# Finished output blocks of a streaming layer: the sample frames' transfers move from ScalarE's queue to SyncE's

## The chip, the cores and the metric

The kernel runs on one core of a Trainium2 chip. The metric is the device time of one execution, in microseconds (us). Engines are named as the profile names them: PE is the matmul engine (PEld its weight loads), DVE the vector engine, ACT the scalar engine (ScalarE), POOL the GpSimd engine, SP the engine that here only issues DMA transfers (SyncE). An ACTq or SPq row is an instruction that one of these sequencers handles itself, such as the issue of a DMA; while ACT's sequencer issues or waits, ACT's computing instructions behind it wait too.

## The reference, cut to what matters

One layer, fp32: a prompt of 512 frames and 64 further frames of a running stream (the sample), 2048 channels each. The time of this change lies in the last matrix product, the down projection, and in writing its result plus the residual to two separate outputs.

```python
def hybrid_layer(x, k_past, v_past, conv_past, ...):
    hn = rmsnorm(x, g_norm1)
    proj = hn @ w_in                                # q, k, v and three convolution groups
    ...                                             # stick-breaking attention, gated convolution
    x = x + mix @ w_out
    h2 = rmsnorm(x, g_norm2)
    x = x + (jax.nn.silu(h2 @ w_gate) * (h2 @ w_up)) @ w_down     # 5632 -> 2048 channels
    return x, k, v, new_conv
...
    yp, kp, vp, cp = hybrid_layer(yp, kp0, kp0, cp0, *wts)                       # 512 frames
    ys, kn, vn, cn = hybrid_layer(ys, cache_k[l], cache_v[l], state_conv[l], *wts)   # 64 frames
```

## The kernel before, in words

Prompt and sample are worked on together, as one block of 576 frames (512 + 64) that lies transposed on the chip: channels on the 128 partitions, frames along the free axis, in two halves of 288 frames. Each fp32 matrix product is made of three matmuls of rounded parts (high times high, low times high, high times low). Weights are loaded raw by DMA from SP's queue (`load_columns`, line 1418), rounded by ACT (line 222, a CAST into `whl`) and their remainder taken by DVE (line 223).

The gate, up and down projections are split into units. A unit multiplies a 2 x 2 block of weights (column halves c = 0, 1) by a 2 x 2 block of frames (halves i = 0, 1) with seven products instead of eight, numbered p_ = 1 to 7 (`run`, `multiply`, line 1532). The partial sums live in PSUM tiles named psy, psw and psx. ACT copies the intermediate state of psy to SBUF (`kept`, line 1542, the tile `part`), and PE's next product into the same psy tile waits for that copy. DVE adds products into the accumulators `acc` (line 1562), POOL adds the copied parts (line 1564).

The down projection has eight column blocks d of 256 output channels and is cut along its 5632 inputs into 37 units (`DOWN`). The list `order` fixes the sequence of products. After each product, the weights of the product four places later are prepared (`AHEAD = 4`). The last eight units finish the column blocks in the order d = 0, 1, 3, 6, 7, 5, 2, 4.

When a unit is the last one of its column block, `store_y` writes the finished accumulators out. It has two ways:

- All column blocks but the last (d = 4) use `turn_blocks`: nine steps after the accumulator is done DVE transposes it in place, 32 x 32 at a time (line 1731), and two steps later `blocks` issues its transfers (line 1720). A full accumulator (576 frames) gives four transfers of 64 KB for the prompt (line 1720, on SP's queue) and four of 8 KB for the sample (the same line, on ACT's queue), one for each group of 32 partitions. Column block 5 has its halves apart: the first half gives four of 36 KB, all prompt, the second four of 28 KB for the prompt and four of 8 KB for the sample. Each transfer moves pieces of 128 bytes.
- The last unit (d = 4) uses `work`: PE transposes the accumulator (lines 1739 and 1742), ACT copies it back (lines 1744 and 1748), and the transfers go out by SP's queue, with the remaining rows by ACT's queue (lines 1700, 1702, 1750, 1755).

From the last up unit on, the program order of ACT, DVE, SP and POOL is the written one, that of PE from the start: each engine works through its own list in order, and an instruction that waits holds everything behind it on that engine. On SP's list the transfers of line 1720 stand between the loads of weights (line 1418) and of hidden activations; on ACT's list they stand between the CASTs of line 222 and the copies of line 1542.

Of the kernel before, what the change touches and what calls it, by code (L numbers as in the profile page):

```python
# [17 lines left out]
TP = 512  # L18
# [76 lines left out]
def tile_hybrid_stream_step(  # L95
# [6 lines left out]
    nc = tc.nc  # L102
# [5 lines left out]
    yp, ys = y_prompt[0], y_sample[0]  # L108
# [151 lines left out]
    def misc(name):  # L260
        return ps_z.tile([P, 512], F32, tag="misc", name=name, bufs=2)
# [219 lines left out]
    t1 = tc.alloc_tile_pool(name="t1", bufs=1, reuse_waits="tile", side="left")  # L481
    dg = t1.tile([P, 5, P], F32, tag="vtok", name="dg")
    for i in range(5):
        n = P if i < 4 else TS
# [692 lines left out]
    for k_, (n, p_) in enumerate(corder):  # L1177
# [7 lines left out]
        if n == NCU - 1 and p_ in (6, 7, 4):  # L1185
            q = {6: 1, 7: 2, 4: 3}[p_]
            t = bt["pool"].tile([P, NH, 2, HALF], F32R, tag=f"t{q}", name=f"forms{q}")
# [430 lines left out]
    for d, v in visits.items():  # L1618
        n = next(a for a, b in zip(v, v[1:]) if a >= NGU + 10 and b >= a + 4)
# [70 lines left out]
    def store_y(n, c, i):  # L1690

        d = UNITS[n][1]
        src, cs, f0 = acc[d, c, i], slice((2 * d + c) * P, (2 * d + c + 1) * P), HALVES[i][0]
        r = HALF - 2 * P

        def put(f, ap, q=nc.sync):

            rows, n_p = ap.shape[0], max(min(TP - f, ap.shape[0]), 0)
            if n_p:
                q.dma_start(out=yp[f : f + n_p, cs], in_=ap[:n_p])  # L1700
            if n_p < rows:
                q.dma_start(out=ys[f + n_p - TP : f + rows - TP, cs], in_=ap[n_p:])

        lone = (d, c) not in both
        k0 = 0 if lone or i == 0 else r
        rest = None
        if lone:
            rest = src[:, 2 * P :], f0 + 2 * P
        elif (d, c) in one:
            rest = both[d, c].rearrange("p i t -> p (i t)")[:, 2 * P : 2 * P + 2 * r], 2 * P  # L1710
        one[d, c] = i

        def blocks(f, ap):

            n = ap.shape[1]
            n_p = max(min(TP - f, n), 0)
            for y, t0, t1, g, eng in ((yp, 0, n_p, f, nc.sync), (ys, n_p, n, f + n_p - TP, nc.scalar)):
                for q in range(4 if t1 > t0 else 0):
                    b0 = cs.start + 32 * q
                    eng.dma_start(out=y[g : g + t1 - t0, b0 : b0 + 32].rearrange("(b t) c -> t b c", t=32),  # L1720
                                  in_=ap[32 * q : 32 * (q + 1), t0:t1].rearrange("t (b c) -> t b c", c=32))

        def turn_blocks():
            if (d, c) in both:
                if done.setdefault((d, c), i) == i:
                    return
                all_, f = both[d, c].rearrange("p i t -> p (i t)"), 0
            else:
                all_, f = src, f0
            yield 9  # L1730
            nc.vector.transpose(out=all_, in_=all_)
            yield 2
            blocks(f, all_)

        def work():
            yield 4
            po = misc("pot")[:, : 3 * P]
            for q in range(2):
                nc.tensor.transpose(po[:, q * P : (q + 1) * P], src[:, k0 + q * P : k0 + (q + 1) * P], ident)
            if rest:  # L1740
                nr = rest[0].shape[1]
                nc.tensor.transpose(po[:nr, 2 * P :], rest[0], ident)
            ob = src[:, k0 : k0 + 2 * P].rearrange("p (i c) -> p i c", c=P)
            nc.scalar.copy(out=ob, in_=po[:, : 2 * P].rearrange("p (i c) -> p i c", c=P))
            if rest:
                turn[0] += 1
                obs = late["raw"][: 2 * r, 4096 + turn[0] % 4 * P : 4096 + (turn[0] % 4 + 1) * P]
                nc.scalar.copy(out=obs[:nr], in_=po[:nr, 2 * P :])
            if i == 0:
                nc.sync.dma_start(out=yp[: 2 * P, cs].rearrange("(i p) c -> p i c", p=P), in_=ob)  # L1750
            else:
                put(f0 + k0, ob[:, 0, :])
                put(f0 + k0 + P, ob[:, 1, :])
            if rest:
                put(rest[1], obs[:nr], nc.scalar)

        pipe.spawn(work() if n == NU - 1 else turn_blocks())
# [107 lines left out]
```

## Time and profile before

Three runs took 2373.28, 2369.54 and 2368.44 us.

| what | before |
|---|---|
| median of the three runs | 2369.54 us |
| the profiled execution, whole | 2369.07 us |
| its span in the trace | 2367.0 us |
| PE busy in the span | 2340.9 us (99%) |
| DVE, ACT, POOL busy | 82%, 49%, 12% |
| granted clock of PE | 1.0 |
| transfers of line 1720 on ACT's queue | 56 (32 + 12 + 4 + 4 + 4) |

The trace starts its clock with the span; 2.07 us of the profiled execution lie outside it. A row of the timeline gives start, duration, engine, line, operation, what it writes and reads, the count of merged instructions, and in square brackets the idle time of that engine before it and what ended it. A row of waits gives the total, the number and the longest wait.

### The profile page before, as it was taken

The page shows a single profiled execution, that of the slowest core. Times are in us where ns is not written, and L with a number is a line of the kernel's source. Part 1 is how long each engine was busy: PE and PEld are TensorE (multiplying, and loading weights), DVE is VectorE, ACT ScalarE, POOL GpSimd, SP SyncE. Part 2 cuts the span into 40 slices and gives each one's busy share as a digit, 9 for nine tenths or more (in the row PEclk, how much of TensorE's full clock was granted, in tenths as well). Part 3 has the DMA queues.
Part 4 walks back from the last instruction along what each step waited for, and adds up shares of the span by engine and source line. Part 5 has one row for each costly group of instructions (what it writes and reads, how often), then busy time and mean ns, then how long its engine had stood idle before and what let it go on. Part 6 is the DMA issues. An engine that isn't in the chain of part 4 may idle for free.

```text
span 2367.0 us, 43888 instructions
## 1 busy us (share of the span) xinstructions
PE 2340.9 (99%) x17581; PEld 2329.5 (98%) x17581; DVE 1935.3 (82%) x2908; ACT 1156.0 (49%) x2039; POOL 294.5 (12%) x386
## 2 busy tenths in 40 slices
PE   8999999999999999999999999999999999999998
PEld 8999999999999999999999999999999999999998
DVE  7878777788887889888888888888888777887896
ACT  6656655444444555444444444444444444444443
POOL 1011111341111230000000000000000002431221
PEclk9999999999999999999999999999999999999999
DMA  8466544684368654444444444444444936885553
GB/s 259 128 175 169 139 138 112 217 266 126 110 226 227 194 166 154 137 152 136 139 152 135 140 152 134 141 152 133 142 152 132 356 115 208 221 235 199 190 143 85
DMA packets 588804, 395.74 MB, mean 167 GB/s; under 512 B 100030, under 2 KB 577720, under 8 KB 588600
## 3 DMA queue, kind: packets, MB, share of 16 engines
q1 hardware_dynamic: 574776, 375.93, 50.9%
q0 software_dynamic: 8624, 16.22, 3.4%
q8 instruction: 137, 2.24, 0.4%
q10 hardware_dynamic: 5200, 0.79, 0.2%
q14 instruction: 67, 0.55, 0.1%
HBM read 301.45 MB, written 91.44 MB: 166 GB/s over the span
## 4 chain that ended last, share of the span: by engine, by line
PE 89%; DVE 5%; DMA 2%; ACT 2%; issue 1%; POOL 0%; ACTq 0%; SPq 0%; POOLq 0%; DVEq 0%
PE psy L1532 33%; PE psw L1532 16%; PE pj L213 13%; PE psx L1532 8%; PE psy L1036 6%; PE pjo L213 4%; PE psw L1036 3%; PE psx L1036 2%; DVE whl L223 1%; DMA raw_a<-in_w_down_dram 1%; PE po L747 1%; PE z L679 1%; ACT whl L222 0%; PE os L777 0%; DVE whl L1008 0%
## 5 line engine op out<-in xcount | busy, mean ns | idle before, releaser
L1532 PE MATMUL psy<-h_s,whl 128*128 128x288 f32 x2787 | 411.7, 294 | 1.7 <-ACT part L1542 1.7
L213 PE MATMUL pj<-x,whi 128*128 128x288 f32 x1856 | 390.5, 297 | 0.3 <-DVE x L356 0.3
L1532 PEld LDWEIGHTS psy<-h_s,whl 128*128 128x128 f32 x2787 | 383.5, 188 | 2.6 <-ACT part L1542 2.6
L223 DVE TENSOR_TENSOR whl<-raw_a,whl 128x1024 fp32r<-128x1024 f32 (+4 forms) x296 | 318.3, 1076 | 57.3 <-ACT whl L222 55.6
L1532 PE MATMUL psw<-t,whl 128*128 128x288 f32 x2400 | 346.9, 294 | 0.0
L1532 PEld LDWEIGHTS psw<-t,whl 128*128 128x128 f32 x2400 | 327.6, 188 | 0.0
L222 ACT CAST whl<-raw_a 128x1024 fp32r<-128x1024 f32 (+4 forms) x296 | 267.6, 906 | 116.7 <-issue 35.3
L213 PEld LDWEIGHTS pj<-x,whi 128*128 128x128 f32 x1856 | 305.0, 189 | 1.0 <-DVE x L356 0.6
L213 PE MATMUL pj<-x,wlo 128*128 128x288 f32 x928 | 274.5, 296 | 0.1
L223 DVE TENSOR_TENSOR whl<-raw_b,whl 128x1024 fp32r<-128x1024 f32 (+5 forms) x190 | 198.1, 1042 | 68.6 <-ACT whl L222 67.2
L222 ACT CAST whl<-raw_b 128x1024 fp32r<-128x1024 f32 (+5 forms) x190 | 164.9, 871 | 169.6 <-issue 73.1
L1542 ACT COPY part<-psy 128x288 f32<-128x288 f32 x242 | 96.7, 400 | 281.9 <-PE psy L1532 258.4
L1532 PE MATMUL psy<-t2t,whl 128*128 128x288 f32 x1212 | 183.5, 295 | 1.2 <-ACT part L1542 1.2
L1532 PE MATMUL psy<-b22m,whl 128*128 128x288 f32 x1212 | 183.1, 295 | 0.6 <-ACT part L1542 0.6
L213 PEld LDWEIGHTS pj<-x,wlo 128*128 128x128 f32 x928 | 174.9, 188 | 0.7 <-DVE wlo L423 0.3
L1532 PE MATMUL psx<-h_s,whl 128*128 128x288 f32 x1185 | 173.7, 294 | 0.0
L1532 PEld LDWEIGHTS psy<-t2t,whl 128*128 128x128 f32 x1212 | 168.3, 188 | 1.6 <-ACT part L1542 1.4
L1532 PEld LDWEIGHTS psy<-b22m,whl 128*128 128x128 f32 x1212 | 168.1, 188 | 0.9 <-ACT part L1542 0.9
L1532 PEld LDWEIGHTS psx<-h_s,whl 128*128 128x128 f32 x1185 | 162.7, 188 | 0.0
L222 ACT CAST whl<-s 128x1024 fp32r<-128x1024 f32 (+5 forms) x81 | 72.2, 892 | 101.7 <-PE psw L1532 99.4
L1311 POOL DMA_DIRECT2D hid_dram<-form x3 | 2.3, 751 | 947.2 <-DVE form L223 947.2
L1532 PE MATMUL psy<-t,whl 128*128 128x288 f32 x576 | 106.5, 294 | 0.0
(456 smaller groups left out, 4392.5 us busy)
## 6 DMA issues: line engine op xcount, KB each, us to landing
hid_dram<-form SPq DMA_DIRECT2D x147, 288.0 KB, 2.3
raw_a<-in_w_in_dram SPq DMA_DIRECT2D x41, 1024.0 KB, 6.1
raw_a<-in_w_gate_dram SPq DMA_DIRECT2D x22, 1024.0 KB, 6.1
raw_a<-in_w_up_dram SPq DMA_DIRECT2D x22, 1024.0 KB, 5.9
raw_b<-in_w_gate_dram SPq DMA_DIRECT2D x22, 1024.0 KB, 6.7
raw_b<-in_w_up_dram SPq DMA_DIRECT2D x22, 1024.0 KB, 7.0
h_s<-hid_dram SPq DMA_DIRECT2D x10, 2016.0 KB, 12.2
raw_a<-in_w_out_dram SPq DMA_DIRECT2D x16, 1024.0 KB, 5.5
```

Source lines behind the costliest of these rows:

```text
L213: mm(ps, w_[:, k, csl], x_, start=(k == 0 and n == 0), stop=(k == nk - 1 and n == 2))
L222: nc.scalar.copy(out=hi, in_=src)
L223: (lo_eng or nc.vector).tensor_tensor(out=lo, in0=src, in1=hi.bitcast(F32), op=ALU.subtract)
L679: mm(zb[i], a_[:, kk], b_[:, q0:TP], start=(n == 0), stop=False, skip_group_check=True)
L747: mm(po[:, i * P : 512], a_[:, i, :], b_[:, : 512 - i * P], stop=(i == 0 and n == 2), **kw)
L1036: mm(ps, whl[:, w_, j, :], x_, start=(start and j == 0 and q == 0), stop=(j == m - 1 and q == 2), skip_group_check=True)
L1311: q.dma_start(out=hid_dram[fp][2 * n - 2 : 2 * n].rearrange("f p t -> p f t"), in_=t.bitcast(F32))
L1532: mm(ps, whl[:, w_, j, :], x_, start=(start and j == 0 and q == 0), stop=(j == len(xs_) - 1 and q == 2), skip_group_check=True)
L1542: nc.scalar.copy(out=t, in_=st["y"])
```

## The change

In `blocks`, the four transfers of the sample are issued by `nc.sync`, like the four of the prompt and after them, where `nc.scalar` issued them before. Their sizes, shapes and number stay the same. The transfers of `work`, in the last unit, keep their queues.

```diff
         def blocks(f, ap):
 
             n = ap.shape[1]
             n_p = max(min(TP - f, n), 0)
-            for y, t0, t1, g, eng in ((yp, 0, n_p, f, nc.sync), (ys, n_p, n, f + n_p - TP, nc.scalar)):
+            for y, t0, t1, g in ((yp, 0, n_p, f), (ys, n_p, n, f + n_p - TP)):
                 for q in range(4 if t1 > t0 else 0):
                     b0 = cs.start + 32 * q
-                    eng.dma_start(out=y[g : g + t1 - t0, b0 : b0 + 32].rearrange("(b t) c -> t b c", t=32),
-                                  in_=ap[32 * q : 32 * (q + 1), t0:t1].rearrange("t (b c) -> t b c", c=32))
+                    nc.sync.dma_start(out=y[g : g + t1 - t0, b0 : b0 + 32].rearrange("(b t) c -> t b c", t=32),
+                                      in_=ap[32 * q : 32 * (q + 1), t0:t1].rearrange("t (b c) -> t b c", c=32))
```

## The prediction

> **What bounds the kernel now.** I read the page first, then who PE waited for in the last 112 us (where all 56 moved transfers are), then the timeline at those places.
>
> ```profile
> span 2367.0 us, 43888 instructions
> ...
> 2255.00:2326.00 71.00, 70.37 (x533) 70.14 (x531) 62.84 (x86) 28.88 (x48) 14.96 (x14) 1.00 0.58 147
> 2326.00:2367.00 41.00, 32.70 (x234) 30.75 (x234) 23.74 (x39) 14.11 (x31) 8.06 (x8) 0.99 0.27 49
> ...
> PE psy L1532 <- ACT part L1542: 2.8, 4, 1.2
> PE psw L1532 <- DVE acc L1562: 0.6, 1, 0.6
> PE pot L1739 <- POOL acc L1564: 0.2, 1, 0.2
> ```
>
> PE bounds nearly everything. In the two stage rows (window, length, then busy time of PE, PEld, DVE, ACT, POOL) it rests 0.63 us of 71 up to 2326, and that is the beginning of the first stall shown below; the last 41 us hold its idle time. The last three rows say for whom: four waits for ACT's copies `part`, one for DVE, one for POOL. The timeline shows what ACT did before those copies:
>
> ```profile
> 2321.12 4.93 ACTq L1720 DMA_DIRECT2D out_dram<-acc  x8
> 2326.10 0.40 ACT L1542 COPY part<-psy 128x288 f32<-128x288 f32 x1 [4.83 <-DMA out_dram<-acc]
> 2326.55 0.67 PE L1532 MATMUL psy<-t2t,whl 128*128 128x288 f32 x3 [1.18 <-ACT part L1542]
> ...
> 2337.77 2.57 ACTq L1720 DMA_DIRECT2D out_dram<-acc  x4
> 2340.44 0.40 ACT L1542 COPY part<-psy 128x288 f32<-128x288 f32 x1 [2.57 <-PE psw L1532]
> 2340.89 0.66 PE L1532 MATMUL psy<-h_s,whl 128*128 128x288 f32 x3 [0.56 <-ACT part L1542]
> ...
> 2351.20 2.01 ACTq L1720 DMA_DIRECT2D out_dram<-acc  x4
> 2353.31 0.40 ACT L1542 COPY part<-psy 128x288 f32<-128x288 f32 x1 [3.55 <-DMA out_dram<-acc]
> 2353.76 0.67 PE L1532 MATMUL psy<-h_s,whl 128*128 128x288 f32 x3 [0.83 <-ACT part L1542]
> ...
> 2354.26 0.88 DVE L223 TENSOR_TENSOR whl<-raw_a,whl 128x512 fp32r<-128x512 f32 x1 [3.09 <-ACT whl L222]
> 2356.23 0.67 PE L1532 MATMUL psw<-h_s,whl 128*128 128x288 f32 x3 [0.57 <-DVE acc L1562]
> 2357.91 0.40 ACT L1542 COPY part<-psy 128x288 f32<-128x288 f32 x1 [3.27 <-DMA out_dram<-acc]
> 2358.36 0.66 PE L1532 MATMUL psy<-h_s,whl 128*128 128x288 f32 x3 [0.28 <-ACT part L1542]
> 2359.25 0.44 PE L1739 MATMUL pot<-ident,acc 128*128 128x128 f32 x2 [0.22 <-POOL acc L1564]
> ```
>
> Each stalled copy stands right behind a group of line 1720 on ACT: the copy at 2326.10 starts when the eight issues from 2321.12 end (2321.12 + 4.93 = 2326.05), and the bracket names nothing else that it waited for. The DVE row at 2354.26 sat 3.09 us for a late ACT cast, so the 0.57 behind DVE comes from the same place, and so does the 0.22 behind POOL, which adds the late `part`. ACT's queue is here an obstacle to PE: six places, 1.18 + 0.56 + 0.83 + 0.57 + 0.28 + 0.22 = 3.64 us.
>
> **The change, part by part. ACT loses 56 issues.** Up to 2325 ACT's issues cost PE nothing, so nothing is won there. From then on the six stalls above go. What is late next at these places is not ACT: its copy can follow its sums at once, and DVE (23.74 busy of 41 us) has room. I take 3.6 us off PE's end; the bounds are 0 (something else is as late) and 3.64.
>
> **SP gains 56 issues.** Their price by rows, four issues each:
>
> ```profile
> 2334.10 1.81 ACTq L1720 DMA_DIRECT2D out_dram<-acc  x4
> 2343.30 1.81 SPq L1720 DMA_DIRECT2D out_dram<-acc  x4
> 2351.23 2.10 SPq L1720 DMA_DIRECT2D out_dram<-acc  x4
> L1720 SPq DMA_DIRECT2D out_dram<-acc x40: 315/428/861, 2306.4 to 2359.2; - x40
> DMA to landing us min/median/max: 1.5/1.8/3.7
> ```
>
> An 8 KB issue on ACT costs 1.81 / 4 = 0.45 us, a 36 KB one on SP just as much, a 64 KB one 0.53: the price is per issue. A full accumulator thus holds SP for 2.10 + 1.81 = 3.9 us instead of 2.1, 0.49 an issue. The Trainium skill, "DMA: Bandwidth & Descriptors", section "Issuing engines are not separate DMA queues", says that all queues end in the same 16 DMA engines and a second issuing engine saves only the issuing time, usually small beside the transfer. Here an issue is a quarter of the 1.8 us to landing, so "small" does not hold in a row of eight; taking it as small, the sum would be the whole 3.6 us (the second case below). The transfers themselves (8 KB, 56 of them) I cost at nothing.
>
> Behind these issues on SP stand, first, the next weights:
>
> ```profile
> 2278.61 1.95 SPq L1720 DMA_DIRECT2D out_dram<-acc_t2z  x4
> 2281.85 1.97 SPq L1720 DMA_DIRECT2D out_dram<-acc_m1z  x4
> 2285.55 0.40 SPq L1418 DMA_DIRECT2D raw_a<-in_w_down_dram  x1
> ...
> 2292.93 0.73 ACT L222 CAST whl<-raw_a 128x640 fp32r<-128x640 f32 x1 [2.04 <-DMA raw_a<-in_w_down_dram]
> 2294.87 0.40 ACT L1542 COPY part<-psy 128x288 f32<-128x288 f32 x1 [1.21 <-DMA out_dram<-acc_z]
> 2295.85 0.56 PE L1532 MATMUL psy<-t,whl 128*128 128x288 f32 x3
> ```
>
> This is the tightest of the four such places, since ACT already waits 2.04 us for the load. Two accumulators in a row now take 2278.61 + 2 x 3.9 = 2286.4, so the load goes out at about 2286.5 instead of 2285.55, 1.0 us late, and the cast starts at 2293.9. Without four issues between them the copy follows at once: 2293.9 + 0.7 + 0.4 = 2295.0, ahead of PE's 2295.85. Cost zero, with 0.85 us of cover left; the cover is ACT's freed time. Each further microsecond on SP would go to PE.
>
> Second, the end of the program:
>
> ```profile
> 2354.53 0.39 SPq L1750 DMA_DIRECT2D out_dram<-acc  x1
> 2360.28 0.83 SPq L1700 DMA_DIRECT2D out_dram<-acc  x2
> 2362.19 0.33 SPq L1702 DMA_DIRECT2D out_dram<-acc  x1
> 2362.61 0.39 SPq L1750 DMA_DIRECT2D out_dram<-acc  x1
> 2362.88 0.32 ACTq L1702 DMA_DIRECT2D out_dram<-raw_b  x1
> 2363.41 0.83 SPq L1700 DMA_DIRECT2D out_dram<-acc  x2
> 2364.68 0.33 SPq L1702 DMA_DIRECT2D out_dram<-acc  x1
> ...
> SPq L1720 <- DMA out_dram<-acc: 11.5, 10, 3.8
> SPq L1702 <- DMA out_dram<-raw_b: 1.5, 2, 1.1
> ```
>
> The end is SP's last issue plus landing (2364.68 to 2367.0 is 2.3 us). Column block 2 starts on SP at 2351.23; with the first two stalls gone (1.18 + 0.56) that is 2349.5. SP then has 8 + 1 + 8 issues: 3.9 + 0.45 + 3.9 = 8.25, up to 2357.75. The last seven issues took 0.83 + 0.33 + 0.39 + 0.83 + 0.33 = 2.7 us without their waits, so the last would start at about 2360.2, ahead of ACT's last one (2362.88 - 3.64 = 2359.24) plus its landing. SP is a queue without a gap from 2349.5 on; its backlog just fits behind a PE that is 3.6 us earlier.
>
> But SP does not run free. The two wait rows show SP issues waiting for earlier transfers to land, also for ACT's transfers out of raw_b, whose data they do not touch. I infer a small set of completion marks handed round over both queues in a planned order, about eight transfers deep. SP's last issue now starts 1.80 us after ACT's last (2364.68 - 2362.88), which is such a wait. With SP falling behind ACT, ACT's last transfer stands earlier in the round, and an SP issue further from the end waits for it. It lets go at 2359.24 + 1.80 = 2361.04. With no SP issue behind that one, the last starts at 2361.04 and 3.64 us are won; with all seven behind it, 2361.04 + 7 x 0.45 = 2364.2, and 0.5 us are won. I take four behind it, half way: 2361.04 + 1.8 = 2362.85, that is 1.8 us earlier than 2364.68.
>
> **Sum.** PE 3.6 us earlier, about 1.8 us of it given back in SP's last queue: 2369.07 - 1.8 = 2367.3 for the profiled execution. The median of the runs is 0.47 above that execution: 2369.54 - 1.8 = 2367.7. About 0.2% (4.7 us) is what a measurement of this kernel can tell from no change, so the forecast is "within 0.2%": 2364.8 to 2374.3.
>
> **The rivals.** *The whole gain arrives*: the waits for landings fall away because one queue hands its marks round in its own order (four issues from 2343.30 took 1.81 us with no wait). Then the time is 2369.5 - 3.6 = 2365.9, at best about 2365, if the 2.0 us of waits among the last seven issues shrink too. For it: the waits in SP's rows come from mixing with ACT. Against it: ACT keeps four transfers in the last unit. To pass 0.2% it would need over 4.7 us, more than all stalls named.
>
> *Nothing is won*: SP's last seven issues end where they do now, because an ACT transfer's mark falls into column block 2's second group; ten issues behind the wait instead of four make 2361.04 + 10 x 0.45 = 2365.5, 0.9 us slower: 2370.4. For it: the 3.8 us that one SP issue waited. Against: single waits near the end are 1.1 at most.
>
> *Slower by more than 0.2%*: SP's stores hold back the weights. If an issue on SP cost 0.86 us throughout (the longest in the line-1720 row) instead of 0.49, sixteen would end at 2278.61 + 13.8 = 2292.4, the load would be 6.9 us late, and PE would stall 6.9 - 1.85 = 5 us there (1.85 is the cover before any delay: 0.85 + 1.0), and similarly at a second column pair: 10 us, less the 1.8 won, 2378. Overall it is slower by 4.7 from a step of about 0.68 us on: (0.68 - 0.49) x 16 = 3.0 more at each of three loads, less 0.85 of cover, is 6.5 of stalls. Against it: fours without a wait took 1.81 to 2.10.
>
> *The change does nothing*, because PE is held by another engine at the same six places: 2369.5. Little speaks for it; DVE's 0.57 is the only wait not named ACT or its sequel.
>
> **How the numbers follow.** The forecast, 0.5 to 3 us won, has 0.44. The whole gain has 0.27, of which 0.08 beyond 0.2%. Nothing won, to 3 us lost, and no effect, have 0.16 together. The slow case has 0.13. So faster 0.08, same 0.79, slower 0.13. For 8 in 10 the range runs from 2364.9 (the full gain, a little more) to 2371.5 (2 us lost, for loads a little late); the likeliest case alone is 2366.5 to 2369.
>
> **What would show it.** Right: no line-1720 rows on ACT; the `part` copies at the four places directly after PE's sums, and PE's waits for `part` gone; loads of line 1418 about 1 us later behind eight-issue groups and no new PE stall before 2326; SP issuing without a gap from about 2349.5, and the time from PE's last product to the end of the span longer than before. Wrong: SP waits of 2 us and more inside eight-issue groups, PE waiting for `whl` or `part` behind a late load, or an end within 4.5 us of PE's last transposes, which is the full gain.

## The result, and the profile after

The changed kernel took 2376.01 us (median of 9 runs, 2373.75 to 2379.44). The kernel before, run beside it and counted with the three runs shown above, took 2371.63 us (9 runs, 2368.44 to 2373.89). The medians are 4.4 us apart. The ratio of the runs is 1.0022, with a 95% interval of 1.0013 to 1.003, so the change is slower, by a small amount that is clear of the noise. The forecast was 2367.7 us, 1.8 us below before. So 2.1 of the 8.3 us by which it missed are in the starting point (the three runs shown lay low), and 6.2 are the wrong sign of the effect.

Where the time lies is read by stage first. These rows are the stages of the profiled execution of the changed kernel (2375.7 us, span 2373.9): window, length, then busy time and number of instructions of PE, PEld, DVE, ACT and POOL, and at the end the granted clock, the DMA share and GB/s.

```profile
0.00:2255.00 2255.00, 2237.53 (x16809) 2227.89 (x16810) 1848.99 (x2784) 1112.61 (x1960) 268.16 (x364) 1.00 0.55 170
2255.00:2326.00 71.00, 69.31 (x522) 68.84 (x521) 61.12 (x84) 28.96 (x48) 15.33 (x14) 1.00 0.53 136
2326.00:2374.00 48.00, 33.47 (x254) 32.91 (x252) 27.40 (x43) 14.42 (x31) 9.06 (x9) 0.89 0.30 59
```

The first row of the kernel before:

```profile
0.00:2255.00 2255.00, 2237.80 (x16816) 2228.58 (x16817) 1848.72 (x2784) 1113.04 (x1961) 271.45 (x364) 1.00 0.55 170
```

Up to 2255, where no moved transfer has been issued, PE had done 16809 matmuls; before it had done 16816. At 0.13 us a matmul (70.37 us for 533 in the second row of before) this execution was 0.9 us behind when it came to the change. SP's last load ahead of the first moved transfer says the same (2259.01, before 2258.05). This is called the late start below, and is not counted as the change's own. In the second stage PE now rests 1.7 us, where it rested 0.63. In the third its busy time is in order; the stage is simply longer. (The granted clock of 0.89 in that row belongs to the time behind PE's end: it is 1.00 from 2326 to 2360.)

For whom PE waits from 2255 on (total, times, longest):

```profile
PE psy L1532 <- ACT part L1542: 1.7, 2, 1.3
PE pot L1739 <- DVE acc L1562: 0.3, 1, 0.3
```

The six stalls of the last 41 us (3.64 us) are gone, as the prediction said, and PE's last transposes end at 2359.8 instead of 2362.1, in spite of the late start. PE's last row after, and before:

```profile
2359.51 0.27 PE L1742 MATMUL pot<-ident,acc 128*32 128x128 f32 x1
```

```profile
2361.88 0.27 PE L1742 MATMUL pot<-ident,acc 128*32 128x128 f32 x1
```

Two new stalls stand further ahead, and the timeline shows what made them (start, duration, engine, line, operation; in brackets the idle time before it and what ended it):

```profile
2284.78 5.09 SPq L1720 DMA_DIRECT2D out_dram<-acc_m1z  x8
2290.28 0.40 SPq L1418 DMA_DIRECT2D raw_a<-in_w_down_dram  x1
...
2296.29 0.73 ACT L222 CAST whl<-raw_a 128x640 fp32r<-128x640 f32 x1 [4.44 <-DMA raw_a<-in_w_down_dram]
2297.36 0.66 PE L1532 MATMUL psy<-t,whl 128*128 128x288 f32 x3 [0.39 <-ACT part L1542]
...
2303.93 0.40 SPq L1418 DMA_DIRECT2D raw_b<-in_w_down_dram  x1
...
2311.66 0.83 ACT L222 CAST whl<-raw_b 128x768 fp32r<-128x768 f32 x1 [5.25 <-DMA raw_b<-in_w_down_dram]
2312.84 0.66 PE L1532 MATMUL psy<-t,whl 128*128 128x288 f32 x3 [1.30 <-ACT part L1542]
```

In the kernel before, the load ahead of these two, and the second of these two, went out as follows:

```profile
2271.66 0.40 SPq L1418 DMA_DIRECT2D raw_b<-in_w_down_dram  x1
...
2299.66 0.40 SPq L1418 DMA_DIRECT2D raw_b<-in_w_down_dram  x1
```

The load that went out at 2285.55 goes out at 2290.28, 4.7 us later (3.8 without the late start), and the next one at 2303.93 instead of 2299.66 (3.3 without it). The one of 2271.66 is already late: it goes out at 2275.07, 2.5 us later without the late start. ACT sits 4.44 and 5.25 us for them, its copy `part` follows the late cast, and PE waits for the copy: 0.39 and 1.30 us.

The larger loss is at the end. SP's waits from 2255 on:

```profile
SPq L1720 <- DVE acc L1731: 12.3, 3, 5.1
SPq L1720 <- DMA out_dram<-raw_b: 12.2, 3, 10.3
```

and the last 20 us of SP's and ACT's issues, with PE's last transposes between them:

```profile
2353.10 0.36 ACTq L1700 DMA_DIRECT2D out_dram<-raw_b  x1
...
2354.57 8.92 SPq L1720 DMA_DIRECT2D out_dram<-acc  x15
...
2358.07 0.32 ACTq L1702 DMA_DIRECT2D out_dram<-raw_b  x1
...
2359.26 0.41 PE L1739 MATMUL pot<-ident,acc 128*128 128x128 f32 x2 [0.31 <-DVE acc L1562]
...
2363.59 0.39 SPq L1750 DMA_DIRECT2D out_dram<-acc  x1
2364.08 4.04 SPq L1720 DMA_DIRECT2D out_dram<-acc  x8
2368.21 0.84 SPq L1700 DMA_DIRECT2D out_dram<-acc  x2
2369.10 0.42 SPq L1702 DMA_DIRECT2D out_dram<-acc  x1
2369.62 0.39 SPq L1750 DMA_DIRECT2D out_dram<-acc  x1
2370.11 0.90 SPq L1700 DMA_DIRECT2D out_dram<-acc  x2
2371.06 0.42 SPq L1702 DMA_DIRECT2D out_dram<-acc  x1
```

Once, SP stands 10.3 us for a transfer out of `raw_b`, whose data it does not touch. It goes on at 2354.57, 1.5 us after ACT issued its first transfer of the last unit (2353.10). Behind it SP still has 15 + 1 + 8 + 2 + 1 + 1 + 2 + 1 = 31 issues. The row of fifteen holds another 1.9 us of standing, for ACT's second and third transfers (2358.07 and 2359.54). Without that pause the 31 issues take 16.9 - 1.9 = 15.0 us, 0.48 each, and SP ends 11.7 us after PE. From PE's end to the end of the span it is 14.1 us; before it was 4.9.

What SP stood for can be read from the records of the transfers in the trace. Each record names the semaphore that the transfer raises when it lands; these are the completion marks of the prediction. In the last 170 us SP's and ACT's transfers take eight of them in turn, numbers 101 to 108, and the record of an issue (or of the wait just ahead of it) names the same number among what it waits for. SP's issues at 2339.20 and 2339.68 have 106 and 108. The 107 between them was dealt to ACT's first transfer of the last unit, which went out at 2353.10, more than 13 us later. The next holder of 107 is SP's issue at 2354.57, and so SP waits. In the kernel before, that transfer of ACT's stands in the round ahead of SP's last 13 issues, and the next holder of its mark is ACT's own second transfer. In the changed kernel it stands ahead of SP's last 38.

### The profile page after: what moved, and what is told of

Read it like the earlier page. It is cut to its first block, busy times and chain, and to the rows that moved or that the text cites. A ratio compares the mean times of both kernels' runs of the same rounds, so it can differ in the third digit from the quotient of the medians.

```text
span 2373.9 us, 43888 instructions
## 1 busy us (share of the span) xinstructions
PE 2340.3 (99%) x17581; PEld 2329.6 (98%) x17581; DVE 1937.5 (82%) x2908; ACT 1156.0 (49%) x2039; POOL 292.6 (12%) x386
## 4 chain that ended last, share of the span: by engine, by line
PE 89%; DVE 4%; DMA 3%; ACT 2%; issue 1%; POOL 0%; SPq 0%; ACTq 0%; DVEq 0%; POOLq 0%
PE psy L1532 34%; PE psw L1532 17%; PE pj L213 12%; PE psx L1532 8%; PE psy L1036 6%; PE pjo L213 4%; PE psw L1036 3%; PE psx L1036 1%; DMA raw_a<-in_w_out_dram 1%; DMA raw_a<-in_w_down_dram 1%; PE po L747 1%; DVE whl L1008 1%; PE z L679 0%; DVE whl L223 0%; PE os L777 0%
## 6 DMA issues: line engine op xcount, KB each, us to landing
h_s<-hid_dram SPq DMA_DIRECT2D x10, 2016.0 KB, 12.2
```

## The experiments

Two theories, and each run takes one cause away. *The marks*: SP's issues wait for completion marks that are handed round over SP's and ACT's transfers alike, and with SP's long list the mark of one of ACT's transfers in the last unit falls far from SP's end. *The loads*: more issues ahead of each load of weights on SP make the loads late. In the expectations below these are theories A and B; theory C there says that SP simply has too many issues at the end. All runs were timed beside the kernel before on the same chip; where runs of different rounds are compared, each is taken by its distance from the before beside it. In the table, PE's waits are those for `part` and for POOL from 2255 on, SP's are the waits of its issues for ACT's transfers out of `raw_b`.

| run | time, us | before beside it | ratio (95%) | PE's waits | SP's waits | SP's last issue |
|---|---|---|---|---|---|---|
| before | 2369.07 (the profiled execution) | | | 3.0 | 1.8 | 2364.68 |
| the change | 2376.01 | 2371.63 | 1.0022 (1.0013 to 1.003) | 1.7 | 12.2 | 2371.06 |
| rest_pool | 2369.73 | 2371.41 | 0.999 (0.9982 to 0.9999) | 1.2 | none | 2364.14 |
| rest_sync | 2373.09 | 2371.41 | 1.0005 (0.9997 to 1.0014) | 1.2 | none | 2368.94 |
| early_only | 2375.24 | 2371.41 | 1.0017 (1.0008 to 1.0025) | 6.4 | 1.9 | 2371.52 |
| late_only | 2372.9 | 2371.41 | 1.0005 (0.9996 to 1.0014) | none | 11.6 | 2366.32 |
| first_pool | 2375.86 | 2371.16 | 1.0019 (1.0011 to 1.0028) | 1.5 | 11.9 | 2370.04 |
| rest3_pool | 2376.07 | 2370.84 | 1.0021 (1.0012 to 1.003) | 1.8 | 11.7 | 2373.50 |
| late_rest_pool | 2369.77 | 2371.16 | 0.9988 (0.998 to 0.9997) | none | none | 2363.9 |
| weights_first | 2367.65 | 2371.16 | 0.9986 (0.9978 to 0.9995) | none | none | 2362.26 |
| late_pool | 2366.93 | 2371.16 | 0.9982 (0.9973 to 0.9991) | 2.3 | none | 2361.33 |
| late_mix | 2366.71 | 2370.84 | 0.9984 (0.9975 to 0.9993) | 0.2 | none | 2361.28 |

**The marks taken away, in two ways.** In rest_pool ACT's four transfers of the last unit go by POOL's queue, in rest_sync by SP's; all else is as in the changed kernel.

```diff
-                put(rest[1], obs[:nr], nc.scalar)
+                put(rest[1], obs[:nr], nc.gpsimd)       # rest_pool
+                put(rest[1], obs[:nr])                  # rest_sync
```

> The changed kernel, but the four small transfers of the last unit that still go by ScalarE's queue (line 1755, out of raw_b) go by GpSimd's queue. SP's issues stay the same in number and order. Theory A (in the changed kernel SP's queue stands 10.3 us before an issue whose completion mark is held by ScalarE's first raw_b transfer, and everything behind it ends late): with ScalarE out of the round, no SP issue in the tail waits for raw_b; SP's groups of column block 2 start at about 2352 to 2353 in the time of the changed profile, the last issue starts near 2364 to 2365 instead of 2371, and the time falls by 5 to 7 us against the changed kernel, to between 1.5 us faster and 0.5 us slower than the kernel before. Theory B (late weight loads and their PE stalls, 0.39 + 1.30 us, are the loss): the time stays within 1 us of the changed kernel, 4 to 5 us slower than before. Theory C (SP simply has too many issues at the end): also within 1 us of the changed kernel, since SP's issues are the same.

> The changed kernel, but the four raw_b transfers of the last unit go by SyncE's queue too, so that one queue hands out all the marks. SP has four issues more. Theory A: no SP wait for a raw_b transfer; four issues of 0.45 us more than with GpSimd's queue, so about 1.8 us slower than that, 3 to 5 us faster than the changed kernel, between 0.5 us faster and 2 us slower than the kernel before. Theory C (too many issues on SP): slower than the changed kernel by about 1.8 us. Theory B: as the changed kernel.

SP's end in rest_pool:

```profile
2357.12 4.06 SPq L1720 DMA_DIRECT2D out_dram<-acc  x8
2361.28 0.85 SPq L1700 DMA_DIRECT2D out_dram<-acc  x2
2362.17 0.42 SPq L1702 DMA_DIRECT2D out_dram<-acc  x1
2362.70 0.39 SPq L1750 DMA_DIRECT2D out_dram<-acc  x1
2363.18 0.90 SPq L1700 DMA_DIRECT2D out_dram<-acc  x2
2364.14 0.42 SPq L1702 DMA_DIRECT2D out_dram<-acc  x1
```

The same last issues stand 6.9 us earlier than in the changed kernel, SP's waits for `raw_b`'s transfers have gone from 12.2 us to nothing, and the time goes from 4.4 us above before to 1.7 below: 6.1 us. The records give POOL's transfers marks of their own (111, 112, 113 and 118). SP has as many issues as in the changed kernel, so theory C alone does not explain the loss. PE's work is the same up to the stall for the late load, which is still there (1.2 us). That the mixing of the queues is what SP stood for is confirmed by rest_sync: there too no wait for `raw_b` is left. But the four issues are then in SP's row at the end, and 3.4 us are lost against rest_pool, so that the time cannot be told from before. The expectation had 1.8. In the profiled executions SP's last issue is 4.8 us later than in rest_pool, of which 2.5 us are a later start (16786 matmuls by 2255 against 16805). The other 2.3 us are about what four issues cost (1.9 us by the 0.48 above) and a wait of 0.4 us for ACT's copy into `raw_b`.

**Half of the change.** early_only moves the samples of the column blocks d = 0, 1, 3, 6 alone, late_only those of 7, 5 and 2 alone.

```diff
-            for y, t0, t1, g, eng in ((yp, 0, n_p, f, nc.sync), (ys, n_p, n, f + n_p - TP, nc.scalar)):
+            for y, t0, t1, g, eng in ((yp, 0, n_p, f, nc.sync), (ys, n_p, n, f + n_p - TP, nc.sync if d in (0, 1, 3, 6) else nc.scalar)):   # early_only
+            for y, t0, t1, g, eng in ((yp, 0, n_p, f, nc.sync), (ys, n_p, n, f + n_p - TP, nc.sync if d in (7, 5, 2) else nc.scalar)):      # late_only
```

> The change for column blocks 0, 1, 3 and 6 alone (32 transfers moved); blocks 7, 5 and 2 keep ScalarE's queue for the sample. Theory A: the end of the program is as before, the six PE stalls in the tail stay, and only the late weight loads count: PE stalls of about 0.4 and 1.3 us near 2297 and 2312, so 1 to 2 us slower than before. Theory B as the whole cause: 4 to 5 us slower than before. Theory C: no change.

> The change for column blocks 7, 5 and 2 alone (24 transfers moved); blocks 0, 1, 3 and 6 keep ScalarE's queue. Theory A: no PE stall near 2297 and 2312, the six stalls of the tail gone (PE's end about 3.5 us earlier than before), but an SP issue waits several microseconds for a raw_b transfer with some 25 issues of 0.49 us behind it: 1 to 4 us slower than before. Theory B: 2 to 4 us faster than before, since the weights come in time and the six stalls are gone. Theory C: 1 to 4 us slower as well, but with SP issuing without a gap longer than 2 us.

early_only lost 3.8 us, more than expected. PE's and ACT's part of it:

```profile
PE psy L1532 <- ACT part L1542: 6.2, 4, 2.5
```

```profile
2326.67 4.85 ACTq L1720 DMA_DIRECT2D out_dram<-acc  x8
2331.57 0.40 ACT L1542 COPY part<-psy 128x288 f32<-128x288 f32 x1 [4.89 <-DMA out_dram<-acc]
```

The first half has the late loads (two stalls, 0.36 and 1.52 us), and the lateness goes on: ACT's eight issues, which began at 2321.12 before, begin at 2326.67, and the stall behind them is 2.55 us instead of 1.18. Another of 1.77 us follows near the end. The four sum to 6.2, against 2.8 for PE's waits on `part` before. The two longest cost more than their length: behind each of them the trace has a stretch of 3.41 us with the granted clock at 0.5, about 1.7 us of PE's work. The first of these lies in this row:

```profile
2330.00:2340.00 10.00, 7.98 (x48) 7.99 (x49) 6.11 (x9) 3.70 (x7) 1.92 (x2) 0.83 0.36 58
```

PE did 48 matmuls in it, where 78 fit into ten undisturbed microseconds. So the early half costs PE time whose size the change hides, since it takes ACT's late issues away as well. late_only has none of PE's stalls, and its SP stands for `raw_b`:

```profile
SPq L1720 <- DMA out_dram<-raw_b: 11.6, 3, 8.8
```

Its time is 1.5 us above before, which the interval does not tell from zero, though in it PE ends earlier (2357.1) than in the kernel before: what PE won is lost in SP's tail.

**Which of ACT's four transfers holds SP.** first_pool moves the first of them to POOL's queue, rest3_pool the other three.

```diff
-                put(rest[1], obs[:nr], nc.scalar)
+                put(rest[1], obs[:nr], nc.gpsimd if turn[0] == 1 else nc.scalar)       # first_pool
+                put(rest[1], obs[:nr], nc.scalar if turn[0] == 1 else nc.gpsimd)       # rest3_pool
```

> The changed kernel with only the first of the four raw_b transfers of the last unit on GpSimd's queue; the other three stay on ScalarE's. Theory A1 (the 10.3 us wait for that first transfer is the whole loss): about as fast as with all four on GpSimd's queue, 4 to 6 us faster than the changed kernel. Theory A2 (each of ScalarE's transfers holds a mark that an SP issue further on needs; the second one holds that of the first issue of column block 2, the 24th from the end, and lands at about 2359.5 in the time of the changed profile): SP idles before column block 2 until then, the last issue still starts 23 x 0.5 = 11.5 us later, near 2371, and the time is within 1 us of the changed kernel, 3.5 to 5 us slower than the kernel before.

> Beside the kernel after: only ScalarE's first remaining-row transfer of the last unit stays on ScalarE's queue, the other three go by GpSimd's. Theory A2 (the wait for the completion mark of that first transfer, with the 31st SP issue from the end behind it, is what carries the tail): SP still stands some 10 us for raw_b, once; the 31 issues behind it then run free, about 15 us for 31 issues plus 2.9 us to the end of the span, so the span is about 2372.5 and the time within 1 us of the run in which the first transfer alone was moved (about 4 us slower than the kernel before). Rival theory A1 (the later transfers' marks, with 24 issues and fewer behind them, carry it): the wait of 10 us does no harm once they are gone, and the time is that of the run with all four on GpSimd's queue, about 1.5 us faster than before.

The names A1 and A2 mean in each of the two texts what that text says of them. In both runs A2 is what happened.

SP's waits in first_pool, and in rest3_pool:

```profile
SPq L1720 <- DMA out_dram<-raw_b: 11.9, 1, 11.9
```

```profile
SPq L1720 <- DMA out_dram<-raw_b: 11.7, 1, 11.7
```

Either alone is enough for the whole loss: 2375.86 and 2376.07, as slow as the change. With the first transfer gone, SP stands at its next place, 24 issues from its end, until ACT's second transfer has landed, and its last issue is at 2370.04; with only the first left, it stands at the 31st from the end. The two waits lie side by side: the first ends at 2354.57 in the changed kernel, and the seven issues between them are done before the second one ends, so that it would be reached in any case. Taking one cause away and seeing no gain would have acquitted it wrongly.

**The second half and the marks together.** late_rest_pool is late_only with the four transfers on POOL's queue.

> Column blocks 7, 5 and 2 as in the changed kernel (24 transfers on SP), blocks 0, 1, 3 and 6 as before (ScalarE), and the last unit's raw_b transfers on GpSimd's queue. Theory A with B for the early blocks: no late weights, so no PE stall near 2312 (1.17 us with all on SP and raw_b on GpSimd); the six stalls of the tail gone; SP ends its 24 issues of the tail as in that kernel. 1 to 2 us faster than that kernel, 2.5 to 4 us faster than before. If late weights cost nothing in the end: as that kernel, 1.7 to 2.4 us faster than before.

It took 2369.77 us, 1.4 below before, where late_only was 1.5 above: with the wait for `raw_b` 2.9 us are gone. No stall for `part` is left, and the early loads are where they were once the late start of that execution (16795 matmuls by 2255, 2.8 us) is taken off: 2274.53 instead of 2271.66, and so on. But the gain of 1 to 2 us on rest_pool that was expected did not show. rest_pool is 1.7 us below the before beside it, so by these medians taking the late loads away won nothing.

**The loads taken away.** weights_first is rest_pool with one thing more: for d = 0, 1, 3, 6 the sample's four transfers go to SP's list twenty steps after the prompt's, behind the next load.

```diff
-            blocks(f, all_)
+            if d in (0, 1, 3, 6):
+                blocks(f, all_, (0,))
+                yield 20
+                blocks(f, all_, (1,))
+            else:
+                blocks(f, all_)
...
-                put(rest[1], obs[:nr], nc.scalar)
+                put(rest[1], obs[:nr], nc.gpsimd)
```

> All sample transfers on SP and raw_b on GpSimd's queue, but for column blocks 0, 1, 3 and 6 the sample's transfers are handed to SP 20 steps (about 8 us) after the prompt's, behind the next load of weights, instead of right behind the prompt's. Number of issues unchanged. Theory B for the early blocks (SP's longer groups delay the loads): the loads of line 1418 go out within 0.5 us of where they do before, PE's stall of 1.17 us near 2312 is gone, 1 to 2 us faster than with the samples directly behind. If the loads are late for another reason: the stall stays, no difference.

Its loads go out at 2271.59, 2285.47, 2299.36 and 2313.75, within 0.3 us of before, with the same number of issues on SP. (The sample's issues now wait 2.0 and 2.5 us for such a load to land, and no stall of PE follows.) Its second stage:

```profile
2255.00:2326.00 71.00, 71.00 (x539) 71.00 (x538) 64.74 (x88) 30.63 (x50) 18.15 (x16) 1.00 0.57 145
```

PE does not rest at all in it, and the time is 3.5 us below before, 1.8 more than rest_pool. That it was the order on SP, and not the number of its issues, that made the loads late is shown by their times. What they cost is less certain. By the profile it is rest_pool's stall of 1.2 us; by the runs it is 1.8 us here and nothing in late_rest_pool, and medians of some ten runs each leave about 2 us of doubt in such a difference.

**A third queue instead of SP.** late_pool is the kernel before with the samples of d = 7, 5, 2 and the four transfers of the last unit on POOL's queue; late_mix is the same, but the very last group (d = 2, c = 1) goes by SP.

```diff
-            for y, t0, t1, g, eng in ((yp, 0, n_p, f, nc.sync), (ys, n_p, n, f + n_p - TP, nc.scalar)):
+            for y, t0, t1, g, eng in ((yp, 0, n_p, f, nc.sync), (ys, n_p, n, f + n_p - TP, nc.gpsimd if d in (7, 5, 2) else nc.scalar)):   # late_pool
+            for y, t0, t1, g, eng in ((yp, 0, n_p, f, nc.sync), (ys, n_p, n, f + n_p - TP, nc.sync if (d, c) == (2, 1) else nc.gpsimd if d in (7, 5, 2) else nc.scalar)):   # late_mix
...
-                put(rest[1], obs[:nr], nc.scalar)
+                put(rest[1], obs[:nr], nc.gpsimd)
```

> Blocks 0, 1, 3 and 6 as before; the sample's transfers of blocks 7, 5 and 2 and the raw_b transfers on GpSimd's queue, so that neither ScalarE nor SP issues them. If SP's 24 issues bound the end, SP now has 16 and the end follows PE: 3 to 5 us faster than before. If GpSimd's own issuing holds back its additions into the accumulators (line 1564), PE's transposes of the last unit wait for them: no gain, or up to 4 us slower than before.

> Beside the run with the samples of column blocks 7, 5 and 2 and the remaining rows on GpSimd's queue: the very last group of four (column block 2, second column half) goes by SyncE instead. In that run GpSimd's four issues at 2352.85 held its addition at 2354.99, and PE stood 2.31 us for it. Theory C (an issue costs about 0.5 us on whichever engine has it, and harms only what stands behind it there): PE's wait for POOL falls from 2.3 us to under 0.5, SP has four issues more (2 us) at a place where it idles later anyhow, and the time falls by 1 to 2 us, to 4 to 6 us below the kernel before. Rival: SP's end, which came 1.3 us behind PE's, takes the 2 us, and nothing is won (within 0.7 us of that run).

(Theory C in the last text is another one: the price of an issue on any engine.)

late_pool is 4.2 us faster than before (2366.93 against 2371.16). POOL's row in its last 14 us, and PE's wait:

```profile
2352.85 2.12 POOL L1720 DMA_DIRECT2D out_dram<-acc  x4
2354.99 0.80 POOL L1564 TENSOR_TENSOR acc<-acc,part 128x288 f32<-128x288 f32 x1
```

```profile
PE pot L1739 <- POOL acc L1564: 2.3, 1, 2.3
```

Four issues cost POOL 2.12 us, 0.53 each, and hold its addition as ACT's issues held its copies. Behind that wait, too, the clock is at 0.5 for 3.41 us. In late_mix the wait shrinks, and PE rests nowhere in the 71 us ahead:

```profile
PE pot L1739 <- POOL acc L1564: 0.2, 1, 0.2
```

```profile
2255.00:2326.00 71.00, 71.00 (x540) 71.00 (x539) 65.05 (x87) 31.29 (x53) 17.38 (x19) 1.00 0.56 144
```

The mechanism was right, and the gain of 1 to 2 us did not show in the time: 2366.71 against 2366.93, each 4.1 to 4.2 us below the before beside it. The profiled execution came late to the last stages (16801 matmuls by 2255, late_pool 16819, so 2.4 us by 0.13 us each) and its span is still 0.5 us shorter, which speaks for a gain. The runs do not tell the two apart, and both beat the kernel before and the change.

## Why the prediction was wrong

**PE's stalls: right.** The six stalls went with ACT's issues, as said. Once both new causes are away, weights_first, with all 56 transfers still on SP's queue, is 3.5 us below the before beside it (2371.16 - 2367.65), against the 3.64 in the prediction. The closeness is partly luck: that run also moves ACT's four transfers to POOL, and late_rest_pool, which has none of the six stalls either, is only 1.4 us below.

**SP's price for an issue: right.** 0.49 us was forecast; the 31 last ones took 0.48 each without their pause. But SP's queue ended later than forecast even where it was free. In rest_pool the last issue is at 2364.14, not 2360.2. Of these 3.9 us, 1.5 are a late start of that execution (16805 matmuls by 2255), about 1.2 are the stall for the late load, which the forecast did not have, and about 1.0 are the last 24 issues (11.7 us from 2352.46 on, where the forecast had 10.7).

**The completion marks: the step that failed.** The prediction saw the mechanism, and put the wait at the wrong place: "ACT's last transfer stands earlier in the round, and an SP issue further from the end waits for it ... I take four behind it". It was ACT's first transfer, which let go of the 31st issue from the end, and then the second, which let go of the 24th. With 31 issues at 0.48 us from a release at 2354.57 on, the last one could not start before 2369.0, and it started at 2371.06. (The forecast had 2362.85.) ACT's last transfer, on which the prediction's sum rests, held the mark of the 18th from the end, and SP came to that one too late to wait. Bounds of none and seven, and a rival with ten, were all taken from the row that had the last such wait in before; where ACT's first three transfers stand in the round was not asked. That is what the change alters: the first stands ahead of 38 issues of SP's instead of 13. The round is not the order of time: by it ACT's first transfer comes between SP's issues of 2339.20 and 2339.68, and ACT could send it only at 2353.10. By rest_pool this term is worth 6.1 us, more than the 4.4 lost in all, where the forecast had 1.8. The prediction's sentence "SP issuing without a gap from about 2349.5" fell with it: SP stood idle from 2344.2 to 2354.57.

The rival *nothing won* argued with the right mechanism (a mark further from the end) and stopped at ten; against it was said that "single waits near the end are 1.1 at most", a row of a kernel in which SP and ACT were in step: there SP waited 11.5 us in ten pieces, in the row that the prediction shows, for transfers out of `acc` to land. Two of the signs that the prediction named for being wrong came true: SP's wait of more than 2 us, and PE waiting for `part` behind a late load.

**The loads: right in kind, too small.** One microsecond late was forecast for the tightest load, with 0.85 us of cover left; it was 3.8 (4.7 less the late start of 0.9). Two parts are visible. The first is that the place called the tightest was not the first to slip: the load ahead of it was already 2.5 us late, behind sixteen issues that took 9.28 us, and SP's group of `acc_m1z` then began 2.0 us late (2284.78 instead of 2281.85, less 0.9). That one carried over to the other is argued from this order, not tested. The second is that single issues took far longer than 0.5 us (last section): one of 1.76 us stands among those sixteen and one of 1.62 in the group of `acc_m1z`. The cost was 1.7 us in PE's stalls here (1.2 in rest_pool), and between nothing and 2 us by the runs. The rival *slower through the weights* named this, as a price of 0.86 us on every issue; the price was 0.48 at the end, and part of the delay came from single long ones.

**The price of issuing, and why a mark is waited for.** The Trainium skill, "DMA: Bandwidth & Descriptors", section "Issuing engines are not separate DMA queues", says that a second issuing engine saves only the issuing time, usually small beside the transfer. "Small" does not hold here: spreading the issues over three engines made late_pool 4.2 us faster, with the same transfers (part of that gain is that SP no longer waits for marks of ACT's). What the prediction did not draw on is the section "Why a DMA increments its semaphore by 16 and not by 1" of the same page in the Trainium skill. It says that when two transfers in flight share one semaphore, a wait on it can pass before the first has fully landed, and asks for one semaphore per transfer in flight. No run here shows such a wait passing early; in this kernel, with eight semaphores to hand round, an issue waits until the last holder has landed, as the records show. The 10.3 us are what such a wait comes to when the holder belongs to another queue and is issued late.

## What to carry to other kernels

When transfers move from one queue to another, find out for each of the last issues on the longer queue which earlier transfer holds its completion mark, and when that one is issued: here the longest such wait near the end was 1.1 us before and became 10.3 us when the two queues fell out of step. Take away all such transfers at once when testing for it, because the next one in line hides the gain of removing the first. An issue cost about half a microsecond on each of the three engines (0.45 us on ACT, 0.48 on SP, 0.53 on POOL) and held what stood behind it there, so the question is where each engine has such room. A load that the matmul engine needs belongs ahead of the stores.

## What the runs showed of the hardware

**Single issues on SP took three times as long as the others.** The durations of SP's issues of line 1720 in the changed kernel (minimum, median, maximum in ns, then first and last start):

```profile
L1720 SPq DMA_DIRECT2D out_dram<-acc_z x24: 315/462/1758, 2265.7 to 2297.5; - x24
L1720 SPq DMA_DIRECT2D out_dram<-acc_m1z x8: 315/484/1622, 2284.8 to 2289.4; - x8
```

The same rows before:

```profile
L1720 SPq DMA_DIRECT2D out_dram<-acc_z x12: 315/482/518, 2264.7 to 2294.0; - x12
L1720 SPq DMA_DIRECT2D out_dram<-acc_m1z x4: 316/420/510, 2281.8 to 2283.3; - x4
```

The long one in the first row lies in the two microseconds from 2270.6, and of the DMA queues in that window one has a single transfer of instructions:

```profile
q1 hardware_dynamic: 1019, 0.13, 40.3%
q8 instruction: 1, 0.02, 4.5%
```

The same stands beside the long issue at 2287.8. In the twelve profiles SP has 29 issues of over 1 us from 2262 on, and beside 28 of them a transfer of instructions starts within 0.35 us. A fetch of instructions that SP has to wait for would fit, and also why more issues on SP meet more of them; only the coincidence is shown, and no run tested the cause.

**POOL's transfers did not hold SP up.** The same four transfers that made SP stand 12.2 us from ACT's queue made it stand for nothing from POOL's (rest_pool). The marks in the records say why: POOL's four have 111, 112, 113 and 118, which no transfer of SP's or ACT's has.

**The clock fell behind the longer stalls of PE.** Behind the stalls of 2.55 and 1.77 us in early_only, 1.76 in rest3_pool and 2.31 in late_pool the granted clock was 0.5 for 3.41 us each time, starting within 1.5 us of the stall's end. Behind the stalls of 1.54 us and less in these stages (first_pool's 1.54, early_only's 1.52, the change's 1.30, the 1.18 of before) it stayed at 1.0. Four cases are not a threshold, but they say that a stall can cost up to 1.7 us more than its length.

**The start of the change wanders.** The number of matmuls done by 2255, ahead of anything that differs between the kernels, lay between 16786 and 16819 over these profiles, 4.4 us at 0.13 us each: as much as the whole effect. Single executions of these kernels can be compared only from that point on.
